# Two-layer trunk with a mixture of experts: the norm behind the experts with half of each row summed in PSUM

## The chip, the cores and the metric

The kernel runs on one core of one Trainium2 chip, as a single launch. The metric is device time in microseconds (us); lower is better. The engines are named as in the profile: PE is TensorE (PEld its weight loads), DVE is VectorE, ACT is ScalarE, POOL is GpSimd, SP is SyncE, which here only issues transfers.

## What is computed

1024 tokens of width 1024 run through two layers. Each layer is a mixer (layer 0: RWKV-7 and gated linear attention; layer 1: S5 and HGRN2), a norm, a hierarchical mixture of 32 experts with the best two for each token, and a second norm. All data are float32; matmuls of the large projections use operands split into a high and a low part.

```python
def _layer_norm(x, g, b):
    xf = x.astype(F32)
    mu = jnp.mean(xf, -1, keepdims=True)
    var = jnp.mean(jnp.square(xf - mu), -1, keepdims=True)
    return ((xf - mu) * lax.rsqrt(var + NORM_EPS) * g + b).astype(x.dtype)
...
# every layer:
x <- LN(alpha*x + mixer(x))
x <- LN(alpha*x + hierarchical_moe(x))     # the norm of this change
```

The expert outputs of a token are summed with its two gates: y = g0 * e0(x) + g1 * e1(x).

## The kernel before

The program is written in stages: layer 0's mixer, its output projection and first norm, routing, the experts, the combine; then the same for layer 1. The experts stream 400 MB of weights through SBUF, and write each token's rows to `ybuf` in DRAM by scattering transfers. Behind them stands a loop for overflowing experts (`moe_more`), which runs zero times here, and then `combine` (L1197), the stage of this change.

`combine` goes over eight tiles of 128 tokens. For a tile, SP loads both expert rows of each token (`cy`, 128 x 2 x 1024, L1204, three buffers), and ACT builds two diagonal matrices from the gates (`cdg`, L1209). For each half of the row (512 columns, one PSUM bank) PE multiplies the two diagonals with the two expert rows and adds them in the bank (L1220, four matmuls a tile; each shows as two records in the trace). The banks come from the ring "iv", which has two. DVE adds alpha times the residual `lnh` (L1221, `scalar_tensor_tensor`, a two-step operation with a factor and a tensor). Then the norm: two `bn_stats` (L674), their aggregate (L675), reciprocal root by Ln and Exp on ACT (L676, L677), minus mean times root (L678, one column), (x - mean) * root over 1024 columns on ACT (L683), times g on DVE (L684), plus b on POOL in four quarters (L690). POOL issues the store (L76, 512 KB).

The residual rows are loaded by `combine_loads` ahead of the overflow loop (five tiles; the others follow inside `combine`).

Layer 0's combine takes tiles 4 to 7, then 0 to 3, and stores to `mid`. As each of tiles 4 to 7 is done, `hT_tile` transposes it on PE (L1234, eight 128x128 transposes) and ACT and DVE split it into `hT_hi` (L106) and `hT_lo` (L111), in halves of four. Behind the loop, `s5_input(1)` projects rows 512 to 1023 for layer 1 (L175 to L177, with weights split into `whi` on ACT and `wlo` on POOL, L118), and `hT_tile` runs for tiles 0 to 3, into the same `hT` tiles. Then layer 1 goes on with the projections of rows 0 to 511 (`s5_input(0)`, then a head of HGRN2, whose first operation on DVE is `he`, L1311), and the S5 setup (L1387 to L1503, some hundred small DVE operations on tables of phases and powers), from which POOL multiplies `sBA` (L1530 to L1532) that PE transposes (L1550).

Layer 1's combine takes tiles 0 to 7, stores to the output and is the end of the program; it is called the tail below.

A list scheduler with a fixed cost model sets the order on every engine when the kernel is built. So an edit moves instructions in its neighbourhood too; each engine runs its list strictly in order.

## Time and profile before

| | us |
|---|---|
| runs | 2884.76, 2887.45, 2890.49 |
| median | 2887.45 |
| profiled execution | 2887.3 |
| its span, first to last instruction | 2885.5 |
| PE busy in it | 2670.9 (93%) |
| DVE busy | 2100.3 (73%) |
| ACT busy | 1586.0 (55%) |
| POOL busy | 819.5 (28%) |

The mean granted clock of PE is 0.951 of full speed. Shares are over the whole program; the expert stages move 378 to 385 GB/s and are bound by their weights, while the stages of this change have other limits. Layer 0's combine lies between 1511 and 1571 us, layer 1's between 2820 and 2885.5 us. An instruction's row in the trace has its start, its duration, and in square brackets how long the engine had been idle and what released it.

### The profile page before, as it was taken

Reading aid. Unit: us, or ns where it says so; the run is one execution under the profiler, and the core shown is the slowest. Engines: PE = TensorE matmul, PEld = TensorE weight load, DVE = VectorE, ACT = ScalarE, POOL = GpSimd, SP = SyncE. Lnnn points to the kernel's source line nnn. Section 1 sums busy time; section 2 is a strip of 40 time slices with the busy share of each in tenths; the row PEclk is TensorE's granted clock in tenths of the full one; section 3 lists DMA queues with packets and bytes.
Section 4 is the critical chain, followed back from the end, with each engine's and each line's share of the span. In section 5 each row is a group of like instructions: output and inputs, shape, how many; then the busy total and the mean of one; then the engine's idle time right before and its main releaser. Section 6 shows DMA issues by size and latency. Waiting matters only on the chain.

```text
span 2885.5 us, 41351 instructions
## 1 busy us (share of the span) xinstructions
PE 2670.9 (93%) x15348; PEld 1980.4 (69%) x15348; DVE 2100.3 (73%) x3228; ACT 1586.0 (55%) x2292; POOL 819.5 (28%) x991
## 2 busy tenths in 40 slices
PE   8999999999897999999988788789997999999994
PEld 6777776766685677777764667678776677777772
DVE  5775447764357899999967568886445899999985
ACT  4343333333333788888864333334533788888872
POOL 5333323323400211111105455462320111111104
PEclk9999989999897999999999889899898999999998
DMA  3111221101354999999967221122443999999985
GB/s 112 31 38 34 62 74 38 30 28 48 128 174 178 373 379 378 378 376 380 385 250 232 88 62 45 56 67 77 140 150 134 355 379 381 382 382 378 380 309 191
DMA packets 234644, 581.57 MB, mean 202 GB/s; under 512 B 48110, under 2 KB 156743, under 8 KB 185287
## 3 DMA queue, kind: packets, MB, share of 16 engines
q1 hardware_dynamic: 212294, 518.04, 50.1%
q0 software_dynamic: 22144, 60.85, 6.0%
q8 instruction: 122, 2.00, 0.3%
q14 instruction: 84, 0.68, 0.1%
HBM read 541.99 MB, written 52.43 MB: 206 GB/s over the span
## 4 chain that ended last, share of the span: by engine, by line
issue 36%; PE 32%; DVE 10%; POOL 8%; DMA 2%; ACT 2%; POOLq 0%; SPq 0%; DVEq 0%; ACTq 0%
POOL xg L970 4%; PE bpj L176 4%; PE bpj L177 4%; PE bpj L175 4%; PE bgs L533 3%; POOL ybuf L1034 2%; PE bpj L729 2%; PE bpj L730 2%; PE bpj L728 2%; PE biv L425 1%; PE bpp L785 1%; PE bpo L182 1%; PE biv L1220 1%; PE by L571 1%; PE by L572 1%
## 5 line engine op out<-in xcount | busy, mean ns | idle before, releaser
L111 DVE TENSOR_TENSOR mlo<-raw,mhi 128x1024 fp32r<-128x1024 f32 x768 | 921.8, 1222 | 105.4 <-ACT mhi L1058 71.2
L1058 ACT ACTIVATE mhi<-raw 128x1024 fp32r<-128x1024 f32 x768 | 806.4, 1059 | 204.5 <-PE bpo L1027 87.1
L118 POOL TENSOR_TENSOR wlo<-wraw,whi 128x256 fp32r<-128x256 f32 x368 | 282.4, 797 | 323.0 <-ACT whi L106 309.3
L175 PE MATMUL bpj<-hT_hi,whi 128*128 128x512 f32 x736 | 306.2, 416 | 12.7 <-DVE hq L588 11.8
L970 POOL DMA_INDIRECT xg<-hdram,gi x64 | 135.4, 2116 | 632.0 <-PE by L982 600.9
L177 PE MATMUL bpj<-hT_hi,wlo 128*128 128x512 f32 x736 | 305.1, 415 | 4.5 <-POOL wlo L118 4.5
L176 PE MATMUL bpj<-hT_lo,whi 128*128 128x512 f32 x736 | 306.4, 416 | 0.0
L996 PE MATMUL bpj<-mhi,xh 128*96 128x512 f32 x512 | 204.9, 400 | 0.0
L106 ACT ACTIVATE whi<-wraw 128x1024 fp32r<-128x1024 f32 x92 | 97.3, 1057 | 195.4 <-PE bpj L176 140.7
L998 PE MATMUL bpj<-mhi,xl 128*96 128x512 f32 x512 | 204.4, 399 | 0.1
L997 PE MATMUL bpj<-mlo,xh 128*96 128x512 f32 x512 | 204.0, 399 | 0.0
L996 PE MATMUL biv<-mhi,xh 128*96 128x512 f32 x512 | 201.8, 394 | 0.0
L997 PE MATMUL biv<-mlo,xh 128*96 128x512 f32 x512 | 201.6, 394 | 0.0
L998 PE MATMUL biv<-mhi,xl 128*96 128x512 f32 x512 | 201.6, 394 | 0.0
L175 PEld LDWEIGHTS bpj<-hT_hi,whi 128*128 128x128 f32 x736 | 142.5, 194 | 47.0 <-DVE hq L588 13.1
L1034 POOL DMA_INDIRECT ybuf<-yo,si x64 | 60.2, 940 | 385.1 <-ACT yo L1033 375.4
L177 PEld LDWEIGHTS bpj<-hT_hi,wlo 128*128 128x128 f32 x736 | 142.0, 193 | 34.8 <-POOL wlo L118 6.7
L176 PEld LDWEIGHTS bpj<-hT_lo,whi 128*128 128x128 f32 x736 | 142.0, 193 | 30.0 <-issue 3.8
L998 PEld LDWEIGHTS bpj<-mhi,xl 128*96 128x96 f32 x512 | 84.1, 164 | 38.0 <-DVE xl L111 1.4
L729 PE MATMUL bpj<-wol,oyh 128*128 128x512 f32 x256 | 105.8, 413 | 4.2 <-POOL wol L118 4.2
L997 PEld LDWEIGHTS bpj<-mlo,xh 128*96 128x96 f32 x512 | 84.2, 164 | 36.5 <-issue 0.2
L996 PEld LDWEIGHTS bpj<-mhi,xh 128*96 128x96 f32 x512 | 84.1, 164 | 35.9 <-issue 0.2
(617 smaller groups left out, 5686.7 us busy)
## 6 DMA issues: line engine op xcount, KB each, us to landing
raw<-in_moe_w_dram SPq DMA_DIRECT2D x384, 1024.0 KB
wraw<-in_ab_w_in_dram SPq DMA_DIRECT2D x50, 512.0 KB
wraw<-in_cd_w_in_dram SPq DMA_DIRECT2D x40, 512.0 KB
cy<-ybuf SPq DMA_DIRECT2D x16, 1024.0 KB
oyr<-ydram SPq DMA_DIRECT2D x16, 512.0 KB
hdram<-or POOLq DMA_DIRECT2D x16, 512.0 KB, 2.9
lnh<-hdram SPq DMA_DIRECT2D x16, 512.0 KB
ydram<-go POOLq DMA_DIRECT2D x16, 256.0 KB, 2.7
```

What stands on the lines that cost most here:

```text
L111: self.keep(self.nc.vector.tensor_tensor(lo, src, hi.bitcast(F32), op=OP.subtract))
L118: lo_engine.tensor_tensor(lo[:, s], src[:, s], hi[:, s].bitcast(F32), op=OP.subtract)
L175: nc.tensor.matmul(dst, wh[:, k, :], xh[:, k, :], start=(k == 0), stop=False)
L176: nc.tensor.matmul(dst, wh[:, k, :], xl[:, k, :], start=False, stop=False)
L177: nc.tensor.matmul(dst, wl[:, k, :], xh[:, k, :], start=False, stop=(k == KT - 1))
L729: nc.tensor.matmul(p, yh[:, k, :], wl[:, ds_], start=False, stop=False)
L970: self.nc.gpsimd.indirect_dma_start(out=xg[:CAP, :], out_offset=None, in_=hdram, in_offset=bass.IndirectOffsetOnAxis(ap=gidx, axis=0), bou ...
L996: self.keep(self.nc.tensor.matmul(p, xh[:, k, :], wh, start=(k == 0), stop=False))
L997: self.keep(self.nc.tensor.matmul(p, xh[:, k, :], wl, start=False, stop=False))
L998: self.keep(self.nc.tensor.matmul(p, xl[:, k, :], wh, start=False, stop=(k == KT - 1)))
L1034: return nc.gpsimd.indirect_dma_start(out=ybuf, out_offset=bass.IndirectOffsetOnAxis(ap=sidx, axis=0), in_=y, in_offset=None, bounds_check ...
L1058: self.keep(self.nc.scalar.activation(hi, src, AF.Copy))
```

## The change

Half 0 of each row gets its residual in PSUM: a fifth matmul with the diagonal matrix `alpha` (identity times alpha, built by one DVE operation in `combine_loads`) adds alpha times `lnh` to the bank. Only half 1 keeps the sum on DVE. `bn_stats` reads half 0 from PSUM. The norm's application becomes two DVE operations for each half: (x - mean) * g, which for half 0 reads PSUM, and that times the root plus b. The ACT pass L683, the one-column L678, the product L684 and POOL's additions L690 are gone from this norm. The banks come from a ring "cb" of six. The load of `cy` and the store are each split into column halves. The first norm of the layers keeps its form (`norm_apply` loses its POOL branch, which that norm didn't use; its call loses the argument).

```diff
@@ -671,26 +671,20 @@
         mv = pool.tile([128, 2], F32, tag="lnmv", bufs=2, name="lnmv")
         rs = pool.tile([128, 2], F32, tag="lnrs", bufs=2, name="lnrs")
         for q in range(2):
-            nc.vector.bn_stats(st[:, q, :], r[:, 512 * q:512 * q + 512])
+            nc.vector.bn_stats(st[:, q, :], r[q] if isinstance(r, list) else r[:, 512 * q:512 * q + 512])
         nc.vector.bn_aggr(mv, st)
         nc.scalar.activation(rs[:, 0:1], mv[:, 1:2], AF.Ln, bias=self.eps)
         nc.scalar.activation(rs[:, 0:1], rs[:, 0:1], AF.Exp, scale=-0.5)
+        if isinstance(r, list):
+            return rs, mv
         nc.vector.scalar_tensor_tensor(rs[:, 1:2], mv[:, 0:1], -1.0, rs[:, 0:1], op0=OP.mult, op1=OP.mult)
         return rs
 
-    def norm_apply(self, r, rs, g, b, out, engine=None):
+    def norm_apply(self, r, rs, g, b, out):
         nc = self.nc
         nc.scalar.activation(r, r, AF.Identity, scale=rs[:, 0:1], bias=rs[:, 1:2])
         nc.vector.tensor_tensor(r, r, g, op=OP.mult)
-        if engine is not None:
-            engine.tensor_tensor(out, r, b, op=OP.add)
-            return
-        for i in range(0, D, D // 4):
-            s = slice(i, i + D // 4)
-            nc.gpsimd.tensor_tensor(out[:, s], r[:, s], b[:, s], op=OP.add)
-
-    def layer_norm(self, pool, r, g, b, out):
-        self.norm_apply(r, self.norm_stats(pool, r), g, b, out)
+        nc.vector.tensor_tensor(out, r, b, op=OP.add)
 
     def rows(self, ap, i):
 
@@ -1180,6 +1174,8 @@
 
     def combine_loads(self, l, order, pool, hdram):
         a = self.a
+        self.alpha = pool.tile([128, 128], F32, name="alpha")
+        self.nc.vector.tensor_scalar(self.alpha, self.ident, ALPHA, None, op0=OP.mult)
         g = self.bcast_row(pool, a["ln2_g"][l], "ln2g")
         b = self.bcast_row(pool, a["ln2_b"][l], "ln2b")
         H = {}
@@ -1196,12 +1192,16 @@
 
     def combine(self, l, order, pool, loads, gate, ybuf, dst, hook):
         nc, a = self.nc, self.a
+        V = nc.vector
         g, b, H, more = loads
         yv = ybuf.rearrange("(j t) d -> j t d", j=2)
         pre = None
+        self.rings["cb"] = "cdefgh"
         for i in order:
             y = pool.tile([128, 2, D], F32, tag="cy", bufs=3, name="cy")
-            nc.sync.dma_start(y, yv.rearrange("j (i p) d -> i p j d", p=128)[i])
+            for q in range(2):
+                s = slice(512 * q, 512 * q + 512)
+                nc.sync.dma_start(y[:, :, s], yv.rearrange("j (i p) d -> i p j d", p=128)[i, :, :, s])
             more()
             h = H[i]
             dg = pool.tile([128, 2, 128], F32, tag="cdg", bufs=2, name="cdg")
@@ -1213,15 +1213,25 @@
                         ins = self.s5_sin(ins)
                     pre = nc.scalar.preload_act_table_set("natural_log_exp_and_others")
                     self.behind(pre, ins)
+
+            r = []
             for q in range(2):
                 s = slice(512 * q, 512 * q + 512)
-                p = self.bank("iv")
+                p = self.bank("cb")
+                if q == 0:
+                    nc.tensor.matmul(p, self.alpha, h[:, s], start=True, stop=False)
                 for j in range(2):
-                    nc.tensor.matmul(p, dg[:, j, :], y[:, j, s], start=(j == 0), stop=(j == 1))
-                nc.vector.scalar_tensor_tensor(h[:, s], h[:, s], ALPHA, p, op0=OP.mult, op1=OP.add)
+                    nc.tensor.matmul(p, dg[:, j, :], y[:, j, s], start=(q == 1 and j == 0), stop=(j == 1))
+                if q:
+                    V.scalar_tensor_tensor(h[:, s], h[:, s], ALPHA, p, op0=OP.mult, op1=OP.add)
+                r.append(h[:, s] if q else p)
             with self.tc.issue_after(pre.ins):
-                self.layer_norm(pool, h, g, b, h)
-            self.store(self.rows(dst, i), h)
+                rs, mv = self.norm_stats(pool, r)
+                for q, x in enumerate(r):
+                    s = slice(512 * q, 512 * q + 512)
+                    V.scalar_tensor_tensor(h[:, s], x, mv[:, 0:1], g[:, s], op0=OP.subtract, op1=OP.mult)
+                    V.scalar_tensor_tensor(h[:, s], h[:, s], rs[:, 0:1], b[:, s], op0=OP.mult, op1=OP.add)
+                    self.store(self.rows(dst, i)[:, s], h[:, s])
             hook(i, h)
 
     def hT_tile(self, hi, lo, x, at):
```

The change moves instructions. The first place is DVE at the end of the tail, the last two tiles. Before (`biv` is the PSUM bank, `ln2g` the factor g):

```order
L684 TENSOR_TENSOR lnh_25457<-lnh_25457,ln2g 128x1024
L675 BN_AGGR lnmv<-lnst 128x2
L1221 SCALAR_TENSOR_TENSOR lnh_25520<-lnh_25520,biv 128x512
L678 SCALAR_TENSOR_TENSOR lnrs<-lnmv,lnrs 128x1
L1221 SCALAR_TENSOR_TENSOR lnh_25520<-lnh_25520,biv 128x512
L674 BN_STATS lnst<-lnh_25520 128x6 x2
L684 TENSOR_TENSOR lnh_25489<-lnh_25489,ln2g 128x1024
L675 BN_AGGR lnmv<-lnst 128x2
L678 SCALAR_TENSOR_TENSOR lnrs<-lnmv,lnrs 128x1
L684 TENSOR_TENSOR lnh_25520<-lnh_25520,ln2g 128x1024
```

With the change (`bcb` is the bank, `lnmv` holds mean and variance, `lnrs` the root):

```order
L1226 SCALAR_TENSOR_TENSOR lnh_25515<-lnh_25515,bcb 128x512
L1232 SCALAR_TENSOR_TENSOR lnh_25485<-bcb,lnmv,ln2g 128x512
L1232 SCALAR_TENSOR_TENSOR lnh_25485<-lnh_25485,lnmv,ln2g 128x512
L1233 SCALAR_TENSOR_TENSOR lnh_25485<-lnh_25485,lnrs,ln2b 128x512 x2
L674 BN_STATS lnst<-bcb 128x6
L674 BN_STATS lnst<-lnh_25515 128x6
L675 BN_AGGR lnmv<-lnst 128x2
L1232 SCALAR_TENSOR_TENSOR lnh_25515<-bcb,lnmv,ln2g 128x512
L1232 SCALAR_TENSOR_TENSOR lnh_25515<-lnh_25515,lnmv,ln2g 128x512
L1233 SCALAR_TENSOR_TENSOR lnh_25515<-lnh_25515,lnrs,ln2b 128x512 x2
```

The sum of the last tile now stands ahead of the four operations of the tile before it, and its own statistics behind them.

The second place is PE at the start of layer 0's combine, from the end of the overflow loop. Before:

```order
L1153 REGISTER_ALU
L1153 COMPARE_AND_BRANCH
L1153 UNCONDITIONAL_BRANCH
L1220 MATMUL biv<-cy,cdg 128x512 x11
L1234 MATMUL bpj<-ident,lnh_13886 128x128 x8
L1220 MATMUL biv<-cy,cdg 128x512 x5
L1234 MATMUL bpj<-ident,lnh_13888 128x128 x8
L1220 MATMUL biv<-cy,cdg 128x512 x4
L1234 MATMUL bpj<-ident,lnh_13890 128x128 x8
```

With the change:

```order
L1147 REGISTER_ALU
L1147 COMPARE_AND_BRANCH
L1147 UNCONDITIONAL_BRANCH
L1222 MATMUL bcb<-lnh_13888,alpha 128x512
L1222 MATMUL bcb<-lnh_13890,alpha 128x512
L1222 MATMUL bcb<-lnh_13892,alpha 128x512
L1224 MATMUL bcb<-cy,cdg 128x512 x9
L1244 MATMUL bpj<-ident,lnh_13888 128x128 x8
L1224 MATMUL bcb<-cy,cdg 128x512 x3
L1222 MATMUL bcb<-lnh_13894,alpha 128x512
L1224 MATMUL bcb<-cy,cdg 128x512 x3
```

Three of the `alpha` matmuls, which need no `cy`, come first; nine instead of eleven `cy` matmuls then stand ahead of the first tile's transposes. In the tail two `alpha` matmuls come first, and no transposes are there.

The third place is DVE behind layer 0's combine. Before, a stretch far inside the S5 setup (the tables `s5co`, `s5si` and phases `s5pq`), where `hT_lo` of tiles 0 to 3 stands:

```order
L1502 SCALAR_TENSOR_TENSOR s5pq_15295<-s5pq_15295 128x32
L1503 TENSOR_TENSOR s5pq_15295<-s5t_15260,s5t_15261 128x32
L1490 TENSOR_TENSOR s5t_15260<-s5co_15256,s5pq_15295 128x256
L111 TENSOR_TENSOR hT_lo<-bpj,hT_hi 128x4x128
L1491 TENSOR_TENSOR s5t_15261<-s5si_15257,s5pq_15295 128x256
L1473 COPY s5ph_15262<-s5pq_15295 128x64
L1492 TENSOR_TENSOR s5co_15256<-s5t_15260,s5t_15261 128x32x8
L111 TENSOR_TENSOR hT_lo<-bpj,hT_hi 128x4x128 x2
L1493 TENSOR_TENSOR s5t_15260<-s5co_15256,s5pq_15295 128x256
L1494 TENSOR_TENSOR s5t_15261<-s5si_15257,s5pq_15295 128x256
L111 TENSOR_TENSOR hT_lo<-bpj,hT_hi 128x4x128 x2
```

With the change, the end of the norm and the first operations of the S5 setup (`s5sg`):

```order
L674 BN_STATS lnst<-lnh_14238 128x6
L675 BN_AGGR lnmv<-lnst 128x2
L1232 SCALAR_TENSOR_TENSOR lnh_14238<-bcb,lnmv,ln2g 128x512
L1232 SCALAR_TENSOR_TENSOR lnh_14238<-lnh_14238,lnmv,ln2g 128x512
L1233 SCALAR_TENSOR_TENSOR lnh_14238<-lnh_14238,lnrs,ln2b 128x512 x2
L135 COPY glub<-biv 128x4
L111 TENSOR_TENSOR hT_lo<-bpj,hT_hi 128x4x128 x7
L1397 MEMSET s5sg 64x1
L1398 MEMSET s5sg 64x1
```

Seven of the eight `hT_lo` of tiles 0 to 3 moved from inside the S5 setup to ahead of it; the eighth stands seven instructions further on. PE's transposes of `sBA`, which stood between the two transpose groups of tile 0, moved behind the first head's first matmuls.

## Rows read from the trace of the kernel before

**Rows 1.** Table by stretch; columns as its first line says, times in us.

```profile
core 0: us, PE busy (x) PEld busy (x) DVE busy (x) ACT busy (x) POOL busy (x), PEclk, DMA share, GB/s
...
1571.00:1600.00 29.00, 17.71 (x83) 14.06 (x81) 28.34 (x76) 8.39 (x13) 23.40 (x31) 0.84 0.39 126
...
2829.40:2833.00 3.60, 3.60 (x5) 1.54 (x6) 0.00 (x0) 0.00 (x0) 0.00 (x0) 0.50 1.02 418
2833.00:2850.00 17.00, 15.97 (x38) 6.89 (x37) 16.02 (x28) 8.61 (x21) 7.41 (x10) 1.00 0.85 309
...
2877.00:2885.50 8.50, 0.00 (x0) 0.00 (x0) 0.00 (x0) 0.00 (x0) 0.00 (x0) 0.50 0.14 56
```

**Rows 2.** Timeline, start of the tail: start, duration, engine, line, operation, count.

```profile
2824.35 1.39 SPq L1204 DMA_DIRECT2D cy<-ybuf  x3
...
2829.38 5.06 PE L1220 MATMUL biv<-cy,cdg 128*128 128x512 f32 x7 [10.57 <-DMA cy<-ybuf]
...
2833.17 0.69 DVE L1221 SCALAR_TENSOR_TENSOR lnh<-lnh,biv 128x512 f32<-128x512 f32 x1 [20.37 <-PE biv L1220]
```

**Rows 3.** Timeline, end of the tail.

```profile
2861.78 1.02 PE L1220 MATMUL biv<-cy,cdg 128*128 128x512 f32 x2
...
2864.16 0.68 DVE L1221 SCALAR_TENSOR_TENSOR lnh<-lnh,biv 128x512 f32<-128x512 f32 x1
...
2864.76 1.28 DVE L674 BATCH_NORM_STATS2 lnst<-lnh 128x6 f32<-128x512 f32 x2
2864.83 2.77 POOL L690 TENSOR_TENSOR lnh<-lnh,ln2b 128x256 f32<-128x256 f32 x4
2865.95 2.74 DVE L684 TENSOR_TENSOR lnh<-lnh,ln2g 128x1024 f32<-128x1024 f32 x1
...
2868.62 0.20 DVE L675 BATCH_NORM_AGGREGATE lnmv<-lnst 128x2 f32<-128x12 f32 x1
...
2870.88 1.75 DVE L684 TENSOR_TENSOR lnh<-lnh,ln2g 128x1024 f32<-128x1024 f32 x1 [1.31 <-ACT lnh L683]
...
2875.76 0.56 POOL L76 DMA_DIRECT2D out_dram<-lnh  x1 [0.30 <-POOL lnh L690]
```

**Rows 4.** Groups of the tail, 2820 to 2886: busy us, mean ns, idle before.

```profile
L684 DVE TENSOR_TENSOR lnh<-lnh,ln2g 128x1024 f32<-128x1024 f32 x8 | 12.3, 1542 | 1.3 <-ACT lnh L683 1.3
```

**Rows 5.** Groups of VectorE, whole program: operations with a column operand.

```profile
L580 DVE SCALAR_TENSOR_TENSOR go<-go,glp,ptmp 128x512 f32<-128x512 f32 x8 | 6.1, 768 | 35.8 <-ACT ptmp L579 35.8
...
L233 DVE SCALAR_TENSOR_TENSOR k<-bpj,rwp,k 128x511 f32<-128x511 f32 x8 | 6.0, 746 | 7.3 <-ACT k L232 7.2
```

**Rows 6.** Timeline of TensorE, start and end of layer 0's combine.

```profile
1519.57 1.19 PE L1220 MATMUL biv<-cy,cdg 128*128 128x512 f32 x1 [14.20 <-DMA cy<-ybuf]
...
1560.63 1.88 PE L1220 MATMUL biv<-cy,cdg 128*128 128x512 f32 x4
```

**Rows 7.** Timeline of TensorE behind layer 0's combine.

```profile
1591.43 1.12 PE L1550 MATMUL bpp<-ident,sBA 128*128 128x128 f32 x4 [5.54 <-POOL sBA L1532]
...
1605.16 1.09 PE L1234 MATMUL bpj<-ident,lnh 128*128 128x128 f32 x4 [10.91 <-DVE hT_lo L111]
1606.47 2.31 PE L1234 MATMUL bpj<-ident,lnh 128*128 128x128 f32 x8 [0.22 <-DVE hT_lo L111]
...
1612.72 0.79 PE L175 MATMUL bpj<-hT_hi,whi 128*128 128x512 f32 x1
```

**Rows 8.** Timeline of VectorE and GpSimd behind layer 0's combine.

```profile
1570.84 0.06 DVE L1387 MEMSET s5sg<- 64x1 f32 x1
...
1571.57 5.41 DVE L1459 COPY s5ph<-s5co 128x32 f32<-128x32 f32 x1
...
1574.11 2.83 POOL L690 TENSOR_TENSOR lnh<-lnh,ln2b 128x256 f32<-128x256 f32 x4
...
1619.10 0.42 DVE L1495 TENSOR_TENSOR ssi<-st,st 128x256 f32<-128x256 f32 x1
1645.73 0.69 DVE L1311 TENSOR_SCALAR he<-bpj 128x512 f32<-128x512 f32 x1 [26.20 <-PE bpj L177]
```

More of the change, by code (lines that the diff above doesn't have):

```diff
@@ L788, in finish @@
             nc.vector.scalar_tensor_tensor(L[:, i, :], p[:, :36], rs[:, 0:1], t, op0=OP.mult, op1=OP.add)
-            self.norm_apply(h, rs, g, b, h, nc.vector)
+            self.norm_apply(h, rs, g, b, h)
             self.store(self.rows(hdram, i), h)
```

## Prediction

> **What bounds the kernel now.** I read the table by stretch first, then the timeline at both ends of the last combine, then the groups of that stretch, and last the waits of TensorE behind the first combine. The program has two combines: layer 0's, with layer 1 behind it, and layer 1's, which ends the program ("the tail").
>
> The tail. TensorE starts 10.57 us late, released by the first cy load [rows 2]; from 2829.4 to 2833.0 the granted clock is 0.50 (the 1.2 GHz level), then 1.00 (2.4 GHz) [rows 1]. From 2833.0 to 2850.0 TensorE is busy 15.97 and VectorE 16.02 of 17.00 us: both are nearly full. The last matmul group begins at 2861.78 and takes 1.02 us [rows 3], so TensorE ends at 2862.80. What follows is a chain of 13 us: the second sum (2864.16), a 2.74 us L684 of the tile before, the aggregate of its statistics (2868.62), Ln, Exp, L678 and L683, its own L684 (2870.88), four GpSimd additions like those at 2864.83 (2.77 us), the store at 2875.76 [rows 3]. In the last 8.5 us no engine computes: the store lands and the program ends [rows 1].
>
> The first combine. TensorE waits 14.20 us for cy, starts at 1519.57 and has its last four combine records at 1560.63 + 1.88 = 1562.5 [rows 6]. Then projections for rows 512 to 1023 of layer 1 run. VectorE starts the S5 setup at 1570.84. TensorE waits 5.54 us for GpSimd's sBA and 10.91 us for VectorE's hT_lo [rows 7], because hT_lo of tiles 0 to 3 stands behind most of that setup. So the projections of rows 0 to 511 start at 1612.72 [rows 7], and `he`, the first gate of a head, follows at 1645.73 after VectorE idled 26.20 us [rows 8]. TensorE is the bound there, and VectorE has 26 us of slack, but behind the transposes and not ahead of them.
>
> **Part 1, the tail.** *Matmuls.* Two records take 1.02 us [rows 3] and four 1.88 [rows 6], so a record more is 0.43 and an instruction (two records) 0.857 us. Added: 8 instructions, 6.9 us here. The order shows two of them ahead of any cy, inside the 10.57 us wait: free. TensorE so runs 38 x 0.857 = 32.6 us from the first half of cy. That half: in the stretch with 418 GB/s [rows 1] 0.5 MB is 1.25 us, so it may land at 2829.38 - 1.25 = 2828.1. Bounds: no gain at all (a completion that costs the same for a half) and 2.5 us (half of the 5.0 us from issue to start, [rows 2]); I take 1.25. The slow clock: two instructions at 0.50 took until 2833.17, some 3.8 us [rows 2], against 1.7; over the 3.6 us of that stretch it costs 1.8, and I allow 0 to 3.4 us, taking 1.0, since two added matmuls run earlier. TensorE ends at 2828.1 + 32.6 + 1.0 = 2861.7 (2860.7 to 2865.4).
>
> A rule speaks against the halves. The Trainium skill, "SBUF — State Buffer", section "Summary: rules for kernel authors", advises one DMA rather than several for a transfer that DMA bounds. By it the first half would not come earlier, and TensorE would end 1.25 us later in each combine; no row here shows halves.
>
> *VectorE.* Per tile before: two sums of 0.68, two bn_stats (1.28 together), 0.20, a one-column L678 and one L684 [rows 3]. After: one sum, two bn_stats, 0.2, four 128x512 operations with column operands. Such operations took 0.746 (PSUM input) and 0.768 us (SBUF) [rows 5]; successive starts lie closer than that (2864.16 to the next operation at 2864.76), so I count 0.66 each. The sum is 5.2 us by durations and 4.6 by starts. Bounds of a new operation: 0.60, the pitch of the plain sum, and 0.77. Eight tiles: 8 x 4.6 = 36.8 from 2830.0 gives 2866.8; by 5.2 it would be 2871.6.
>
> *After the last matmul*, by the order shown: the sum (0.72 with its wait), four operations of the tile before (2.64), two statistics (1.2), 0.2, then 4 x 0.68 = 2.7. Ln and Exp lie beside the two operations that need only the mean. Total 7.4, so 2869.1; the second store half is issued 0.3 later, as it was before, at 2869.4 against 2875.76: **gain 6.3**. The removed ACT pass, L678 and the four GpSimd additions all lay on this path. The bounds are 3 (VectorE at 5.2 us a tile, slow clock) and 8.5. The store is half as large; I count nothing for it (0 to 0.6 us).
>
> One row decides whether VectorE gets its clean price. L684 took 2.74 us at 2865.95 while a GpSimd L690 ran from 2864.83 for 2.77 us; the mean of the eight is 1542 ns [rows 3, 4], while a sum of half the width takes 0.68 at a pitch of 0.60, so some 1.22 is the clean price. If the cause is the overlap, the change takes it away, since GpSimd computes nothing more there. If it were something else, the four new operations would cost 0.75 x 1542/1220 = 0.95 each, and the end would come 1.1 us later in the last tile. The Trainium skill, "SBUF — State Buffer", section "Who interferes with whom", says that a VectorE operation with two SBUF inputs and a GpSimd one that reads SBUF lock each other out for a whole instruction; the row agrees. By that rule, three of the four new operations and the whole S5 setup can still be held by GpSimd's weight splits in layer 0.
>
> **Part 2, the first combine.** 40 instructions instead of 32, three of them ahead of cy. 37 x 0.857 + 4 x 2.31 for a tile's eight transposes [rows 7] = 40.9 us from 1519.57 - 1.25 = 1518.3: 1559.2, plus up to 3.4 of slow clock; before, the same work ended at 1562.5 [rows 6]. Gain 0 to 3.3, taken 1.4, since the clock will cost some of it.
>
> **Part 3, what the planner moves.** This is the largest term and the least sure. All eight hT_lo of tiles 0 to 3 now stand on VectorE right behind the norm and ahead of nearly all of the S5 setup. So the 5.54 us ahead of sBA's transposes and the 10.91 us go: the projections of the second half end near 1591.43 - 5.54 - 1.4 = 1584.5, eight transposes at the pace of 1.25 us a half (five from 1606.47 to 1612.72, [rows 7]) end near 1594.5, and the projections of rows 0 to 511 start there instead of at 1612.72: 18.2 us earlier. What is late next is VectorE: the setup now starts near 1593.5 instead of 1570.84. In the trace it took until 1619.5 [rows 8], 48.7 us. Of these 4.8 were the eight hT_lo, by the plain sum's pitch, and 5.2 a copy of 128x32 that took 5.41 us beside GpSimd's work, an L690 among it [rows 8]: 38.7 are left. At best, were all of it stretched like L684 (1542 against 1220), it is 30.6 and ends at 1624.1; at worst another such collision comes on top, 1637.4. `he` stands behind it on VectorE, and needs the projections, 33.0 us after their start, 1627.5. So `he` falls between 1627.5 and 1637.4; I take 1634, the 38.7 us and a third of a collision. Gain at `he`: 1645.73 - 1634 = 11.7 (8.3 to 18.2), which includes part 2. From there on TensorE is the bound, as before. The S5 block then comes later in the plan, 0 to 4 us either way.
>
> Beside these: 16 more loads and stores on SP and POOL queues (three cy issues took 1.39, 0.46 each [rows 2]) cover themselves behind the load that is waited for; one 128x128 operation builds `alpha` during the MoE. Both nothing.
>
> **Sum.** 2887.3 (the profiled execution, 0.15 below the median) - 6.3 - 11.7 = 2869.3, and 2869.5 against the median.
>
> **Rivals.**
> *A, the moved work is given back.* The S5 setup loses its 26.20 us of slack and becomes the bound. GpSimd's sBA products wait for it, as they did by VectorE's late tables before [rows 7], and stand in GpSimd's queue ahead of a weight split that the projections of rows 0 to 511 need; with the setup 23 us later and collisions beside, `he` comes at 1643 to 1648. For it: VectorE was busy 28.34 of 29 us there [rows 1]. Against: half of that stretch lay beside additions that are gone. Only the tail remains: 2887.4 - 6.3 = 2881.
> *B, slower: the new operations run at the price of the disturbed L684,* 2.74 us for 1024 columns [rows 3], 1.37 each. A tile then takes 0.68 + 1.28 + 0.2 + 5.5 = 7.6 us, the tail 61 from 2830.0, so its end comes at 2891, 15 us later; in layer 0, 61 and sixteen hT_lo at 0.69 from 1520 hold the setup until 1597 and `he` until 1637.5, a gain of 8. Time: 2887.4 + 15.2 - 8.2 = 2894. In the tail it decides from about 0.9 us an operation. For it: reading a sum twice in PSUM has no row; against: both kinds of operand in [rows 5].
> *C, VectorE is not late at all.* `he` comes with the projections, at 1627.5: 2887.4 - 6.3 - 18.2 = 2863.
> *D, the halves bring nothing* and the clock stays low: tail gain 3, `he` at 1637.4: 2887.4 - 3 - 8.3 = 2876.
>
> **How the numbers follow.** Forecast 0.50, A 0.20, C 0.12, D 0.10, B 0.08. What a measurement can tell from no change is 0.2%, 5.8 us: faster means below 2881.7, slower above 2893.2. Forecast, C and D lie below (0.72), A on both sides (0.10 faster, 0.09 same, 0.01 slower), B above: faster 0.82, same 0.09, slower 0.09. The range begins below C, with the tail's better bound (8.5) and 4 us of the S5 block: 2857; it ends at 2883, above A by part of its tail bound; outside are B and the worse part of A.
>
> **What would show it.** Right: in the tail, L1222 before cy, last sum near 2861 less the earlier gain, 7.4 us from there to the last operation, no GpSimd addition; behind the first combine, L1244 waits for hT_lo of under 3 us, projections of rows 0 to 511 some 18 us earlier, `he` some 12 us. Wrong: TensorE waiting over 10 us for weight splits or for `he` to free a bank (A), L1232 or L1233 at over 0.9 us (B), or a tail that has its last VectorE operation more than 42 us behind the first half of cy.

## The result, and the profile after

| | before | with the change |
|---|---|---|
| runs, us | 2884.76 to 2890.49 (4) | 2855.03 to 2861.39 (4) |
| median, us | 2888.52 | 2860.31 |
| profiled execution: time, span | 2887.3, 2885.5 | 2855.03, 2852.9 |
| mean granted clock | 0.951 | 0.961 |

The ratio is 0.9895 (95% interval 0.9883 to 0.9907): 28.2 us by the medians, against 18.0 forecast. Ahead of the first combine the change adds one operation, the one that builds `alpha`; the two profiles come to it 3.5 us apart all the same (first `cdg` at 1511.30 and 1507.85), and a second profile of the change at 1509.14. So every reading below counts from the first `cdg` of its own combine, and not from the start.

The tail with the change, its start in the timeline:

```profile
2801.66 3.78 PE L1222 MATMUL bcb<-lnh,alpha 128*128 128x512 f32 x4 [5.76 <-ACT cdg L1209]
...
2806.11 6.41 PE L1224 MATMUL bcb<-cy,cdg 128*128 128x512 f32 x10 [0.67 <-DMA cy<-ybuf]
...
2809.90 0.70 DVE L674 BATCH_NORM_STATS2 lnst<-bcb 128x6 f32<-128x512 f32 x1 [20.06 <-PE bcb L1224]
```

The `alpha` matmuls run at 2801.66, ahead of any cy, and TensorE waits 0.67 us where it waited 10.57 [rows 2]. But the first matmul on cy comes 4.88 us after the first `cdg` (2801.23); before it was 4.89 (2829.38 less 2824.49): the half arrives no earlier. The table by stretch there:

```profile
2803.50:2807.00 3.50, 2.83 (x4) 0.84 (x3) 0.00 (x0) 0.43 (x2) 0.00 (x0) 0.50 0.98 356
2807.00:2824.00 17.00, 17.00 (x38) 7.45 (x37) 12.79 (x22) 3.51 (x12) 2.26 (x4) 0.91 0.96 321
2824.00:2841.00 17.00, 16.84 (x40) 7.16 (x38) 17.00 (x30) 3.20 (x13) 3.49 (x7) 1.00 0.74 272
```

The clock is 0.50 for 3.5 us from 2803.5 and 0.91 in the next stretch, 1.00 only in the last; TensorE has no idle time in 2807 to 2824, and VectorE none in 2824 to 2841. The groups of the new operations in the tail:

```profile
L1233 DVE SCALAR_TENSOR_TENSOR lnh<-lnh,lnrs,ln2b 128x512 f32<-128x512 f32 x16 | 11.3, 746 | 0.0
...
L1232 DVE SCALAR_TENSOR_TENSOR lnh<-bcb,lnmv,ln2g 128x512 f32<-128x512 f32 x8 | 6.0, 744 | 0.1
L1232 DVE SCALAR_TENSOR_TENSOR lnh<-lnh,lnmv,ln2g 128x512 f32<-128x512 f32 x8 | 5.9, 743 | 0.0
```

All three take 743 to 746 ns, near the prices of [rows 5] (746 and 768), with PSUM input or without. The end of the tail:

```profile
2837.24 3.60 PE L1224 MATMUL bcb<-cy,cdg 128*128 128x512 f32 x8
...
2844.35 0.69 DVE L674 BATCH_NORM_STATS2 lnst<-bcb 128x6 f32<-128x512 f32 x1
...
2846.58 0.74 DVE L1232 SCALAR_TENSOR_TENSOR lnh<-lnh,lnmv,ln2g 128x512 f32<-128x512 f32 x1
2847.24 1.41 DVE L1233 SCALAR_TENSOR_TENSOR lnh<-lnh,lnrs,ln2b 128x512 f32<-128x512 f32 x2
2848.28 1.20 POOL L76 DMA_DIRECT2D out_dram<-lnh  x2 [0.66 <-DVE lnh L1233]
```

TensorE ends at 2840.84, VectorE at 2848.65, the last store's issue at 2849.48. That is 48.25 us from the first `cdg`; before, the issue at 2875.76 [rows 3] ended 51.83 us after it: **3.6 us**. From there to the end of the span it takes 3.42 us; before it took 9.18. This **5.8 us** had no place in the forecast, which gave at most 0.6 us to it.

Layer 0's combine, table by stretch, with the change:

```profile
1519.50:1532.40 12.90, 12.90 (x37) 5.94 (x35) 11.31 (x20) 4.05 (x12) 1.17 (x2) 0.99 0.92 309
1532.40:1559.30 26.90, 26.90 (x94) 15.51 (x93) 26.53 (x47) 8.13 (x23) 5.40 (x10) 1.00 0.96 275
```

and before:

```profile
1519.50:1532.40 12.90, 12.74 (x22) 5.20 (x22) 7.01 (x12) 3.02 (x7) 3.00 (x6) 0.76 0.85 307
1532.40:1559.30 26.90, 22.82 (x70) 9.94 (x71) 21.55 (x39) 13.85 (x29) 13.03 (x21) 1.00 0.94 273
```

TensorE is busy all the time where it had gaps. What it waited for in the second stretch before (total, times, longest):

```profile
PE bpj L1234 <- POOL lnh L690: 4.0, 14, 0.6
```

These are the transposes of tiles 4 to 7, which waited for GpSimd's additions of b, quarter by quarter. The change has no such additions.

The clocks of the first stretch (0.99 and 0.76) can't be compared as they stand, since it begins 11.7 us after the first `cdg` with the change and 8.2 us after it before. Counted from `cdg`, the next rows are 8.5 to 11.9 us and 11.9 to 14.9 us with the change, and 11.4 to 14.4 us before and in the run with the tail alone (below), which runs the order of before in layer 0:

```profile
1516.30:1519.70 3.40, 3.37 (x4) 1.51 (x5) 0.00 (x0) 0.00 (x0) 1.92 (x3) 0.51 1.05 392
1519.70:1522.70 3.00, 3.00 (x8) 1.33 (x7) 1.68 (x3) 0.69 (x2) 0.00 (x0) 1.00 0.99 367
...
1522.70:1525.70 3.00, 3.00 (x5) 1.02 (x4) 1.38 (x2) 0.00 (x0) 0.00 (x0) 0.50 0.81 324
...
1522.60:1525.60 3.00, 3.00 (x8) 1.33 (x7) 2.21 (x4) 0.69 (x2) 0.00 (x0) 1.00 0.78 311
```

So with the change, too, the first 3.4 us of matmuls on cy ran at half the clock. The profile of before stayed at 0.50 some 3 us longer, the tail alone did not: that difference is one of the executions and not of the change.

Behind the combine, with the change, in the timelines of TensorE and VectorE:

```profile
1549.98 3.60 PE L1224 MATMUL bcb<-cy,cdg 128*128 128x512 f32 x8
...
1578.00 0.16 DVE L135 COPY glub<-biv 128x4 f32<-128x4 f32 x1 [12.61 <-PE biv L133]
...
1586.24 0.06 DVE L1397 MEMSET s5sg<- 64x1 f32 x1
...
1586.31 0.50 PE L175 MATMUL bpj<-hT_hi,whi 128*128 128x512 f32 x1
...
1624.90 0.43 DVE L1505 TENSOR_TENSOR ssi<-st,st 128x256 f32<-128x256 f32 x1
1625.24 0.68 DVE L1321 TENSOR_SCALAR he<-bpj 128x512 f32<-128x512 f32 x1
```

The combine's last matmul ends at 1553.58, 45.7 us after the first `cdg` (51.2 before; 49.7 and 50.0 in two later profiles with the order of before in layer 0). VectorE then idles 12.61 us ahead of the small copy `glub`, whose matmul stands late on TensorE, splits the transposed tiles, and starts the setup at 1586.24, 78.4 us after `cdg` (59.5 before). The projections of rows 0 to 511 start with it, at 78.5 (101.4). `he` runs at once when the setup's last operation has ended, at 117.4 (134.4): **17.0 us** earlier. In the two later profiles just named (tail alone, half stores alone) it came at 132.4 both times; against them the gain is 15.0.

### The profile page after: what moved, and what is told of

Its sections match the earlier page's. It is cut to its first block, busy times and chain, and to the rows that moved or that the text cites. A ratio compares the mean times of both kernels' runs of the same rounds, so it can differ in the third digit from the quotient of the medians.

```text
span 2852.9 us, 41401 instructions
## 1 busy us (share of the span) xinstructions
PE 2676.2 (94%) x15380; PEld 1984.6 (70%) x15380; DVE 2100.8 (74%) x3246; ACT 1565.3 (55%) x2276; POOL 782.6 (27%) x943
## 4 chain that ended last, share of the span: by engine, by line
issue 36%; PE 32%; DVE 9%; POOL 8%; ACT 2%; DMA 2%; POOLq 0%; SPq 0%; DVEq 0%; ACTq 0%
POOL xg L964 4%; PE bpj L176 4%; PE bpj L175 4%; PE bpj L177 4%; PE bgs L533 3%; POOL ybuf L1028 2%; PE bpj L723 2%; PE bpj L724 2%; PE bpj L722 2%; PE bcb L1224 1%; PE biv L425 1%; PE bpp L779 1%; PE bpo L182 1%; DVE sX L1599 1%; POOL wol L118 1%
## 5 line engine op out<-in xcount | busy, mean ns | idle before, releaser
L175 PEld LDWEIGHTS bpj<-hT_hi,whi 128*128 128x128 f32 x736 | 141.3, 192 | 41.6 <-DVE hq L588 7.6
```

The costliest lines, as they stand in the source:

```text
L175: nc.tensor.matmul(dst, wh[:, k, :], xh[:, k, :], start=(k == 0), stop=False)
```

## Experiments

Each kernel was profiled once and timed in five rounds beside the kernel before. The table has what the sections speak of, in us: `he` and the first head's core (its first matmul `bgs`, L533) from layer 0's first `cdg`; the end of the last store's issue from the tail's first `cdg`; and from there to the end of the span, called the rest. A ratio below 1 is faster than before.

| kernel | ratio to before (95%) | he | core | last issue | rest |
|---|---|---|---|---|---|
| before | 1 | 134.4 | 151.2 | 51.8 | 9.2 |
| the change | 0.9895 (0.9883 to 0.9907) | 117.4 | 133.7 | 48.3 | 3.4 |
| layer 0 alone | 0.9930 (0.9915 to 0.9946) | 117.0 | 133.3 | 52.1 | 9.5 |
| tail alone | 0.9982 (0.9971 to 0.9993) | 132.4 | 149.1 | 48.6 | 9.8 |
| order alone | 0.9953 (0.9937 to 0.9968) | 125.7 | 145.0 | 51.9 | 9.2 |
| whole transfers | 0.9911 (0.9893 to 0.9928) | 116.9 | 133.1 | 46.4 | 9.2 |
| no added matmul | 0.9898 (0.9875 to 0.9922) | 113.8 | 130.1 | 51.5 | 3.4 |
| two banks | 0.9953 (0.9934 to 0.9971) | 129.5 | 146.2 | 51.3 | 3.4 |
| order, additions on VectorE | 0.9939 (0.9922 to 0.9956) | 122.9 | 139.4 | 51.6 | 9.2 |
| late phases | 0.9925 (0.9910 to 0.9941) | 111.6 | 129.6 | 46.6 | 3.4 |
| added matmul in the tail alone | 0.9887 (0.9872 to 0.9902) | 118.3 | 137.8 | 48.1 | 3.4 |
| the same, whole loads | 0.9894 (0.9879 to 0.9909) | 116.5 | 133.1 | 46.3 | 3.8 |
| the change again | 0.9883 (0.9865 to 0.9901) | 117.4 | 133.7 | 48.3 | 3.4 |
| half stores alone | 1.0012 (1.0003 to 1.0021) | 132.4 | 149.1 | 56.7 | 9.8 |

From the first head's core to the tail's first `cdg` there are some 1160 us more; the two profiles of the change itself took 1159.7 and 1166.6 there, so one profile can't place less than 7 us in that stretch. At `he` the three profiles with layer 0 as before differ by 2.0 us. The expectations count a last issue, and the rest, from the start of the last row of issues: 47.1 and 4.6 for the change, 51.3 and 9.7 before.

**Each layer alone.** The other layer's combine is that of before; the second kernel has `if l == 1`.

```diff
+            if l == 0:
...
+            else:
+                nc.sync.dma_start(y, yv.rearrange("j (i p) d -> i p j d", p=128)[i])
...
+                rs = self.norm_stats(pool, h)
+                nc.scalar.activation(h, h, AF.Identity, scale=rs[:, 0:1], bias=rs[:, 1:2])
+                nc.vector.tensor_tensor(h, h, g, op=OP.mult)
...
+                    nc.gpsimd.tensor_tensor(h[:, s], h[:, s], b[:, s], op=OP.add)
+            self.store(self.rows(dst, i), h)
```

> The change in layer 0's combine alone; the tail is as before. Theory (plan and norm in layer 0): 20 us of the gain sit between the first diagonal of layer 0's combine and that of layer 1's (1313.2 us before, 1293.4 with the change), so about 2868.5, 17 to 22 below before. Rival (most of it is in the tail, with its last store): no more than 12 below before.

> The change in layer 1's combine alone; every other engine order is that of before. Theory: 3.6 us by the way from the first diagonal to the last store issue (51.3 to 47.7), and 0 to 6 us more from how the last store ends, since 9.2 us lay behind the end of its issue before and 3.4 in the profile of the change: 2879 to 2885. Rival (the end of the store is chance, its size does nothing): 2885, 3 to 4 below before.

Layer 0 alone gains 0.70%, 20.2 us (15.6 to 24.6), the tail alone 0.18%, 5.2 us (2.0 to 8.4). For layer 0 the theory held and the rival is out. For the tail the time can't tell the theory from the rival, since 3 to 4 us lie within the interval, and the profile speaks for the rival: the chain gave 3.3 us (51.8 to 48.6) and the end nothing. There the rest behind the last issue stayed long, though its stores are halved and its last rows read like those of the change:

```profile
2871.96 1.20 POOL L76 DMA_DIRECT2D out_dram<-lnh  x2 [3.01 <-DVE lnh L1238]
```

Together the two give 25.4, less than the 30.3 and 33.8 us by the two ratios of the change; the intervals are wide, but the short rest of 3.4, which neither kernel has alone, would explain the missing 5 to 8 us.

**The order alone.** The norm of before; the setup is put behind the eighth hT_lo (`lo03`).

```diff
-                    self.s5_setup(sp)
+                    with tc.issue_after(self.lo03.ins):
+                        self.s5_setup(sp)
```

> The norm of before, additions on GpSimd and all, with one rule added: the whole S5 setup stands behind the eighth hT_lo of tiles 0 to 3. Theory (the order is what pays in layer 0): the projections of rows 0 to 511 start some 15 us earlier, he some 10 to 18, total 10 to 18 below before. Rival (the quicker norm pays, the order alone gives the time back on VectorE, since the setup then runs beside GpSimd's weight splits): within 4 us of before.

13.6 us faster (9.2 to 18.2): the rival with at most 4 us is out. The projections of rows 0 to 511 start at 84.0 us instead of 101.4, but the theory's 10 to 18 us at `he` came out as 8.8 (6.7 against the two later profiles). VectorE's timeline, the setup's start and end:

```profile
1598.35 0.06 DVE L1388 MEMSET s5sg<- 64x1 f32 x1
...
1637.96 0.84 DVE L1496 TENSOR_TENSOR ssi<-st,st 128x256 f32<-128x256 f32 x1
1638.73 0.68 DVE L1312 TENSOR_SCALAR he<-bpj 128x512 f32<-128x512 f32 x1
```

The setup starts 85.3 us after `cdg` and takes 40.4, and `he` follows at once. The change has nearly the same order and starts it at 78.4. So of the 15.0 to 17.0 us at `he`, about half is the order and half the norm that ends sooner; without the norm, TensorE's last matmul of the combine came at 50.0, with it at 45.7.

**Whole transfers.**

```diff
-            for q in range(2):
-                nc.sync.dma_start(y[:, :, s], ...)
+            nc.sync.dma_start(y, ...)
...
-                    self.store(self.rows(dst, i)[:, s], h[:, s])
+            self.store(self.rows(dst, i), h)
```

> The change with whole transfers, cy in one load and each tile's store in one. Theory (halves of the load do nothing: the first matmul on cy came 4.88 us after the first diagonal with halves and 4.89 with whole loads): the start of the tail is the same within 0.5 us; the last store is issued no later than 0.4 us after, and carries twice the bytes: 0 to 6 us slower than the change, all of it behind the last store issue. Rival (halves pay at the head of both combines): 2 to 3 us slower, at the first matmul of each.

`he` and core are those of the change. The first matmul on cy comes 5.60 us after the tail's `cdg`, 0.7 later than in the change (the theory allowed 0.5), and the last issue is even earlier (46.4; the reason is shown below, under whole loads). Yet the rest is 9.2 again, and the time 5 to 8 us above the change by the ratios (the intervals overlap in part). Halves of the load don't pay at the head, as the theory had it.

**No added matmul, and only in the tail.** Half 0 is summed on VectorE like half 1, in the first kernel in both layers, in the second in layer 0 (its edit is the one shown).

```diff
-                if q == 0:
+                if l and q == 0:
                     nc.tensor.matmul(p, self.alpha, h[:, s], start=True, stop=False)
```

> The change without the added matmul: both halves are summed on VectorE, the rest as in the change. Theory (matmul and VectorE are balanced at five matmuls a tile): TensorE ends up to 6 us earlier, but VectorE's tile grows from 4.6 to 5.2 us, 42 us for eight from about 8.7 us after the first diagonal, so the last store of the tail is issued near 50.5 us after it (47.1 with the change), and the whole is 2 to 5 us slower than the change. Rival (TensorE bounds the tail, the added 13.7 us of matmuls in both combines cost): 3 to 6 us faster than the change.

> The change with the added matmul in layer 1's combine alone; layer 0's sums both halves on VectorE. Theory (the five matmuls pay where VectorE sets the end, in the tail, and cost where TensorE does, in layer 0): the way from the first diagonal of layer 0's combine to that of layer 1's is that of the kernel without the added matmul (1286.7 us, 1293.4 with the change), the last store of the tail is issued as in the change (47.1 us after the first diagonal): 3 to 7 us faster than the change. Rival (the 6.7 us between the two profiles are scatter from run to run): within 2 us of the change.

Without it the tail's last issue came at 51.5, 3.3 later, near the 3.4 worked out; but layer 0 ran ahead by as much (`he` 3.6 earlier), which the theory had not counted, and the total equals the change instead of 2 to 5 us more. With the matmul in the tail alone the tail was that of the change (48.1), but `he` came at 118.3, on the same order that had given 113.8. The setup took 42.4 us there instead of 38.6, and one operation makes most of the difference, while GpSimd runs four weight splits (1628.20 to 1631.02):

```profile
1627.68 3.62 DVE L1504 TENSOR_TENSOR st<-ssi,s5ph 128x256 f32<-128x256 f32 x1
```

In the change the same operation took 0.41 us. None of the three totals can be told from another, and the rival's word, scatter, is what the second kernel supports. Whether the added matmul pays in layer 0 stays open: without it TensorE's last matmul of the combine comes at 41.6 and 42.3 instead of 45.7, but `he` hangs on the setup.

**The same with whole loads.**

> As the kernel before it, but cy in one load a tile; the stores stay in halves. Theory (halves of the load do nothing for the start, and with whole loads three added matmuls run ahead of the first cy in the tail instead of two): 0 to 1.5 us faster than with halved loads, the last store issue near 45.9 us after the first diagonal, and the gap behind the last store issue stays short (4.6). Rival (halved loads pay): 1 to 3 us slower.

Here three added matmuls run ahead of cy, and TensorE has no pause before it. The table by stretch:

```profile
2805.50:2810.50 5.00, 5.00 (x6) 1.85 (x7) 0.00 (x0) 2.32 (x5) 0.00 (x0) 0.50 0.88 316
2810.60:2824.00 13.40, 13.40 (x33) 5.99 (x33) 10.32 (x18) 2.86 (x10) 1.19 (x2) 1.00 0.99 350
```

The clock is 0.50 for the added matmuls only and 1.00 from the first cy on; the last issue comes at 46.3 instead of 48.1 (its row starts at 45.1, where 45.9 had been expected). In the total it is not to be seen. Three added matmuls are not the condition, though: the kernel with the late phases (below) has the two of the change and a longer pause (1.03 us), and had the full clock at the first cy too, with its last issue at 46.6:

```profile
2820.80:2824.00 3.20, 3.17 (x8) 1.52 (x9) 0.70 (x1) 0.00 (x0) 0.00 (x0) 1.00 1.04 373
```

**Two banks.**

```diff
-        self.rings["cb"] = "cdefgh"
+        self.rings["cb"] = "cd"
```

> The change with a ring of two PSUM banks instead of six. Half 0 then holds its bank until the first operation of the norm's application has read it. Theory (the six banks are needed by the sum in PSUM): TensorE waits for VectorE in each tile, 1 to 2 us of it, so 8 to 16 us slower than the change over both combines, with the first matmul groups and the operations themselves unchanged. Rival (banks do not matter, as before with two): within 2 us of the change.

Some 17 to 20 us slower than the change, by its two ratios, more than the 8 to 16 expected. In layer 0 TensorE's last matmul of the combine came at 61.9 instead of 45.7, in the tail at 46.4 instead of 39.6. Its waits, with what ended them, two rows of layer 0's combine and one of the tail:

```profile
PE bcb L1224 <- DMA cy<-ybuf: 10.2, 3, 6.2
PE bcb L1222 <- ACT cdg L1209: 6.4, 1, 6.4
...
PE bcb L1222 <- DVE lnh L1232: 2.1, 6, 0.4
```

The last row is the bank itself: in six tiles of the tail the added matmul waits for the operation that reads half 0 from its bank. In layer 0 the waits are put down to cy and `cdg`; 6.2 us of the one and all of the other lie ahead of the first matmul on cy. The planner made another order for two banks, with one added matmul ahead of cy and the others in step with VectorE, so the run prices two banks with the order that goes with them. The rival (banks don't matter) is out.

**Order, with the additions on VectorE.**

```diff
-            nc.gpsimd.tensor_tensor(out[:, s], r[:, s], b[:, s], op=OP.add)
+            nc.vector.tensor_tensor(out[:, s], r[:, s], b[:, s], op=OP.add)
```

> The norm of before and the S5 setup behind hT_lo, as in the run with the order alone, but the additions of b on VectorE (four of 128x256 a tile) and none on GpSimd. Theory (VectorE's work per tile sets the norm, GpSimd's collisions are worth some us): a tile takes VectorE about 5.4 us, the tail is bound by it and its last store is issued near 52 us (51.4 with the additions on GpSimd); in layer 0 the S5 setup meets fewer collisions and he comes 1 to 4 us earlier than with the order alone (125.7 us after the first diagonal). In total within 4 us of the order alone. Rival (GpSimd is what the change pays by leaving): 6 to 10 us faster than the order alone, as the change is.

`he` 2.8 us before that of the order alone, the last issue 0.3 before, and 4 us in all: the theory. The rival's 6 to 10 us from GpSimd's leaving are not there (the ratios differ by 4 us and their intervals overlap).

**Late phases.**

```diff
+            with self.tc.issue_after(self.hf_ins.ins):
             for i in range(6):
                 if i < 4:
                     self.phases(co, si, ph, t1, t2, 1 << i)
```

> The change with one more rule: the second half of the S5 setup (the phase tables) stands behind hf of the first head. Theory (he is bound by the S5 setup on VectorE: it came 0.0 us after the setup's end, 39 us after its start, and 5.5 us later than the projections would allow): he at 111.5 to 113 us after the first diagonal (117.4 with the change), the first head's core near 128 (133.7); total 2 to 6 us faster than the change, less what the first S5 block loses by its later tables. Rival (he is bound by the projections): he unchanged, total within 1 us.

`he` in VectorE's timeline:

```profile
1622.56 0.69 DVE L1321 TENSOR_SCALAR he<-bpj 128x512 f32<-128x512 f32 x1 [14.81 <-PE bpj L177]
```

It came at 111.6 us and the core at 129.6, so VectorE's setup did bound `he` in the change, and the projections are next. But the time is 9 to 12 us above the change, where 2 to 6 below had been expected. TensorE's waits from 1640 to 1960 in this kernel

```profile
PE bgs L533 <- DVE gQ L544: 22.4, 11, 8.8
```

and in the change:

```profile
PE bgs L533 <- DVE gQ L544: 12.9, 9, 6.3
```

have 9.5 us more behind `gQ`, an operation on VectorE, which now has the phase tables to do among the first heads' work. A gain at `he` is worth its full size only if VectorE's setup doesn't get later by it.

**Half stores alone.** The kernel before, with the tail's stores halved.

> The kernel before, with only the tail's stores split in halves (GpSimd issues the first half behind two of its four additions); every other engine's order is that of before. Theory (what lies behind the last store issue depends on its size: 9.7 us in five profiles with 512 KB, 4.6 in four of five with 256 KB): the second half is issued 0.6 us later than the whole was, and the gap falls from 9.7 to 4.6: 4 to 5 us faster than before. Rival (the gap does not hang on the size, but on what else ends there): 0 to 1.5 us slower than before.

Slower by 0.12% (0.03 to 0.21). The last tile's L684 and the last issue:

```profile
2875.65 2.87 DVE L684 TENSOR_TENSOR lnh<-lnh,ln2g 128x1024 f32<-128x1024 f32 x1 [1.31 <-ACT lnh L683]
...
2883.59 0.55 POOL L76 DMA_DIRECT2D out_dram<-lnh  x1 [0.30 <-POOL lnh L690]
```

GpSimd now has two issues among its additions, and its chain collides with L684 again (2.87 us). The last issue ends 56.7 us after `cdg`, 4.9 later, and the rest is 9.8. Not all of the 4.9 is the edit's: the clock stayed at 0.50 until 10.9 us after `cdg`, before until 8.5. The size of the last store is not what makes the rest short: the theory fell. The rival's 0 to 1.5 us were too few.

**The change again.**

> The change itself once more, on the chip of the two kernels before it, to compare them with. Its ratio to before should be that of its first timing (0.9883 to 0.9907); in the profile the last store issue near 47 us after the first diagonal and a gap of either 4.6 or some 10 us behind it.

It repeats the first timing, and its `he`, core, last issue and rest to 0.1 us.

## Why the prediction was right, and by how much its terms were off

The way and the range held; four of its terms were of the wrong size. Two of them made the gain smaller than forecast (the half load and the clock, in the tail), two larger (the transposes and the end).

*Part 1.* "It may land at 2829.38 - 1.25": the half landed no earlier. Over all profiles the first matmul on cy came 4.6 to 5.4 us after `cdg` with halved loads and 4.9 to 5.6 with whole ones, 0.2 apart on the average. The rule that was weighed there (the Trainium skill, "SBUF — State Buffer", section "Summary: rules for kernel authors": one DMA rather than several) is the one that this row bears out. The slow clock cost 2.1 us instead of 1.0: 34.73 us from first to last matmul on cy against 32.6. VectorE's prices were right (744 ns, starts 0.66 apart), and from the last matmul to the last operation it took 7.8 against 7.4. Gain on the chain 3.6 instead of 6.3; the missing 2.7 are the half (1.25), the clock (1.1) and the rest of that chain (0.4). One of the signs of being wrong was touched: VectorE's last operation starts 41.8 and ends 42.5 us behind the first matmul on cy, where 42 was the limit.

*The end.* "The store is half as large; I count nothing for it": behind the last issue the time fell by 5.8 us. With it the tail gave 9.3. The prediction read the last 8.5 us before as the store landing; most of it was something else (see the last section), and that it fell was luck.

*Part 2.* "Gain 0 to 3.3, taken 1.4": it was 5.5 against the profile of before (51.2 to 45.7) and 4.0 to 4.3 against the two later ones (49.7, 50.0). The half load and the clock were against it here too: the first matmul on cy came at 8.48 us after `cdg` (8.27 before), and the added matmuls ahead of it brought the clock up only until they paused for cy. The term of the wrong size was "4 x 2.31 for a tile's eight transposes", 9.2 us: with the change the four groups kept TensorE busy for 4.2 us in all. Before they took 7.0, and 4.0 more in waits for GpSimd's additions, which the sum did not look at.

*Part 3.* The steps were right: waits for sBA and hT_lo gone (of L1244's waits for hT_lo, 0.2 to 0.6 us each are left), projections earlier (23.0 us, forecast 18.2), `he` bound by the setup. The setup took 39.1 us (forecast 38.7, in the trace before 48.7 with 4.8 of hT_lo), and started at 78.4 instead of the forecast 82.2 us after `cdg`, because part 2 was too small. So 15.0 to 17.0 at `he` instead of 11.7. The setup's collisions with GpSimd became fewer, but by the order and not by the additions that are gone: the 128x32 copy that took 5.41 us beside them [rows 8] took 0.17 in the change, and 0.19 in the order alone, where the additions had ended 21 us ahead of the setup (1598.35):

```profile
1574.61 2.81 POOL L691 TENSOR_TENSOR lnh<-lnh,ln2b 128x256 f32<-128x256 f32 x4
```

Collisions are not gone, as one of the new operations with two SBUF inputs shows, in the norm's last tile of layer 0, with GpSimd's weight splits running:

```profile
1561.24 2.33 DVE L1232 SCALAR_TENSOR_TENSOR lnh<-lnh,lnmv,ln2g 128x512 f32<-128x512 f32 x1
```

2.33 us instead of 0.74. That is the behaviour which the Trainium skill, "SBUF — State Buffer", section "Who interferes with whom", describes; in the tail, where GpSimd computes nothing, all operations kept their price.

*The rivals.* A (the moved work is given back) didn't occur at `he`; the late phases show that it can, one step further on. B needed operations of 0.9 us. C would have had `he` at 111.5 in place of 117.4. D was half right: the halves of the load bring nothing, and the clock stayed low for a while.

In sum: 15.0 to 17.0 at `he`, 3.6 on the tail's chain and 5.8 behind it make 24.4 to 26.4 of the 28.2 us. That the gain at `he` reaches the tail is not seen in single profiles, which scatter by 7 us there; layer 0 alone, 20.2 us (15.6 to 24.6) faster, supports it.

## What to carry to other kernels

Look in the built order for what a change moves, before pricing what it removes: at `he` the place of eight small operations ahead of a setup was worth about as much as the leaner norm. Compare profiles from a common event, not at equal times, and with a second profile of the same order: here one profile was 2.0 us late by itself. A sum moved into PSUM needs banks for as long as the vector engine reads them; with two, more than half of the gain was gone. An operation that is taken away also ends the waits of others for it, as with the transposes. And an earlier milestone (`he`) is not yet an earlier end, if the work that was pushed behind it is waited for next.

## What the runs showed of the hardware that was not expected

The time from the last store's issue to the end took two values: 3.4 to 3.8 us in all seven profiles with halved stores in both combines, 9.2 to 9.8 us in all seven others, among them those with halved stores in one combine and those in which the last store was the same 256 KB. In the kernel before, the last stretch of the table reads

```profile
2880.00:2885.50 5.50, 0.00 (x0) 0.00 (x0) 0.00 (x0) 0.00 (x0) 0.00 (x0) 0.50 0.00 0
```

so nothing moved in the last 5.5 us, and the end was not held up by the data. The time lies in one record on GpSimd, called DRAIN, at the program's end. It begins with the last store's issue, and the end of the program follows it by 0.8 us. Before and with the change (durations in ns: shortest, median, longest; the longest is the one meant):

```profile
L1790 POOLq DRAIN  x3: 46/120/8920, 2875.7 to 2885.2; - x3
...
L1800 POOLq DRAIN  x3: 46/120/3152, 2848.9 to 2852.6; - x3
```

In the seven short profiles it takes 3.1 to 3.5 us, in the seven long ones 8.9 to 9.6. It goes with the number of packets on GpSimd's queue in the whole program, before

```profile
q0 software_dynamic: 22144, 60.85, 6.0%
```

and with the change:

```profile
q0 software_dynamic: 22400, 60.85, 6.0%
```

22272 (one combine halved) went with the long one. Whether that number is the cause was not tried, and what GpSimd does in this time stays open; it is 5.8 us of the 28.2, and another number of stores elsewhere in a program might bring or cost as much.

TensorE's clock at the first matmuls on cy was not settled by the kernel's order. In the tail the change and the late phases have the same order, with two added matmuls ahead of cy: in the change (both profiles) the clock was 0.50 until 8.5 to 8.7 us after `cdg`, as in before without them (8.5), in the late phases until 4.1 only, and their last issue came 1.6 us earlier. In layer 0 the change's three added matmuls brought it to 1.00 at 5.0 us after `cdg`; TensorE then waited 2.99 us for cy, and from 8.4 to 11.8 us the clock was 0.50 again. So the added matmuls there bought no faster start on cy; the kernels without them reached 1.00 at 11.4 to 11.8 us too, but for two profiles at 14.4 and 14.8.
